# One fp32 product instead of three split products in the RG-LRU block of a two-network kernel

## The chip, the cores and the metric

The kernel runs on one core of one Trainium2 chip, as one program. The metric is the time of one execution in device microseconds (us). Five engines of the core matter here: PE (TensorE, the matrix engine; PEld is its weight load), DVE (VectorE), ACT (ScalarE), POOL (GpSimd), and SP (SyncE), whose queue issues most DMA transfers. Each engine takes its instructions strictly in program order, and semaphores hold one engine until another has done something.

## The reference, cut to what matters

The whole computes two networks one after the other, with 512 rows of 1024 numbers between them: a first block (a state-space mixer and an MLP), then two layers, each a mixer and a mixture of experts (MoE). The change touches the mixer of the very last layer, `mixer_rglru`:

```python
def mixer_rglru(h, w_in, conv_w, conv_b, w_a, b_a, w_x, b_x, lam, w_out):
    gate, xr = jnp.split(h @ w_in, [D_RNN], axis=-1)          # 512x1024 @ 1024x2048
    gate = jax.nn.gelu(gate)
    xr = causal_conv(xr, conv_w) + conv_b                      # 4 taps
    xh = xr.reshape(bsz, t_len, LRU_HEADS, LRU_HEAD_DIM)       # 8 heads of 128
    r = sigmoid(einsum('bthi,hij->bthj', xh, w_a) + b_a)
    i = sigmoid(einsum('bthi,hij->bthj', xh, w_x) + b_x)
    log_a = (LRU_C * r) * log_sigmoid(lam)
    a = exp(log_a)
    b = sqrt(-expm1(2.0 * log_a)) * (i * xr)
    hseq = scan of  h_t = a_t * h_(t-1) + b_t
    return (gate * hseq) @ w_out
```

All inputs and the output are fp32.

## The kernel before

PE takes its operands in two forms here. With plain fp32 operands a product is one instruction in the program. With operands of type fp32r the program first splits each operand into a high part (a rounded copy) and a low part (what is left), and makes three products of the parts, high x high, high x low and low x high (`mm3`, lines 265 to 267; the split of weights is `split`, L293 on ACT for the high part, L297 on DVE or L295 on POOL for the low part). The RG-LRU block works with the split form throughout.

The block lies between the MoE of the layer before it and its own output projection. At the end of that MoE, `over` transposes the first half of the 512 rows (`gT`, PE L400, ACT L402 for the high part `nh`, DVE L404 for the low part `nl`). Then 16 views follow. A view is one column block of 128 outputs by 512 rows: eight products of 128x128 by 128x512 summed in one PSUM bank, over the eight chunks of 1024. The first two views are one item, done in halves, with the other four transposes between the halves (`hook`). Eight views make the recurrent input x (m = 0 to 7) and eight make the gate (m = 8 to 15), in the order that a list sets:

```python
order = [0, 1, 2, 3, 8, 4, 9, 5, 10, 6, 11, 7, 12, 13, 14, 15]
```

After each view its callback `cb(i)` writes instructions for the other engines. For an x view (`cb_x`): a multiply out of PSUM by the row norm `rb`, and the four-tap convolution on DVE (L1746, L1749, three times L1751). `rb` is made once, at the end of the first two views, by `bcast_r` (PE L1669, ACT L1670). Later steps of a view are entered in the list `steps` at its own index plus an offset: `gates(m)`, which makes the two gate products of head m on PE and their Tanh and Exp on ACT; `middle(m)` (three DVE and two POOL operations, L1721 to L1725); `coef` (L1730 to L1736), `scan` (L1741) and `out`, which writes the block's result, split into `mh` and `ml`, for the output projection. `gates(m)` is not run at once but put into `k.fills`: five products steps into the next view its matmuls are written between those of that view, so they stand in PE's queue there. Before `gates` the kernel splits x (`copy_x` on ACT L1758, `sub_x` on DVE L1763).

Weights come by DMA through two buffers of 2 MB (pool `raw`): four chunks of four views each (`cols4`), the gate weights (`loadg`, split in `prepg`, POOL L1700), then two chunks of the output projection. The next chunk is issued when a buffer has been read for the last time; in the kernel before that reader is the split of its last view. Up to three splits are written ahead of their use. The output projection (`out_proj`, `tm_items`) keeps the three-product form, with splits L293 and L297. Behind it come routing and the MoE of the last layer.

Of the kernel before, what the change touches and what calls it, by code (L numbers as in the profile page):

```python
# [21 lines left out]
F32 = mybir.dt.float32  # L22
F32R = mybir.dt.float32r
# [8 lines left out]
P = 128  # L32
D = 1024
SEQ = 512
# [4 lines left out]
KD = D // P  # L39
# [12 lines left out]
GE = 7  # L52
# [9 lines left out]
def dram(ap, offset, dims):  # L62
    return bass.AP(tensor=ap.tensor, offset=ap.offset + offset, ap=dims)
# [54 lines left out]
class Kern:  # L118
# [35 lines left out]
    def pair(self, name, n):  # L154

        x = [self.slot(name, i, (4, n), F32R) for i in range(4)]
        return Rows(x[:2]), Rows(x[2:])
# [1321 lines left out]
class Second:  # L1479
# [175 lines left out]
    def rglru_open(self):  # L1655
        k = self.k
        p = self.np_ = k.open("abn")
        self.nh = p.tile([P, KD, SEQ], F32R, name="nh")
        self.nl = p.tile([P, KD, SEQ], F32R, name="nl")
        self.rb = p.tile([P, SEQ], F32, name="rb")  # L1660
        self.rr = p.tile([P, NB], F32, name="rr")
        self.g1 = k.g_mix2[:, 8:16]
# [9 lines left out]
    def rglru(self):  # L1672


        k = self.k
        v, s, t, g, A = k.v, k.s, k.t, k.g, k.A
        name = "c_w_in_2"
# [14 lines left out]
                k.nc.sync.dma_start(w[:, i], A[n].rearrange("o h i j -> i (o h) j"))  # L1692
            return w
        def prepg():
            w = k.piece(self.wg)
            self.wgh = self.np_.tile([P, 2, 8, P], F32R, name="wgh")
            self.wgl = self.np_.tile([P, 2, 8, P], F32R, name="wgl")
            for i in range(2):
                s.copy(self.wgh[:, i], w[:, i])
                g.tensor_sub(self.wgl[:, i], w[:, i], self.wgh[:, i].bitcast(F32))  # L1700
        W = lambda n, bufs, shape=(SEQ,), dt=F32: self.w.tile([P, *shape], dt, name=n, bufs=bufs)
        st, wait, held = {}, [], []

        def gates(m):
            x, xs = st[m]
            r = []
            for i in range(2):
                p = k.acc()
                k.mm3(p, self.wgh[:, i, m], self.wgl[:, i, m], xs[:, 0], xs[:, 1], True, True)
                o = W(f"r{i}", 2 + 2 * i)  # L1710
                s.activation(o, p, AF.Tanh, scale=0.5, bias=self.hb[:, i, m:m + 1])
                r.append(o)
            t1, t2 = r
            q = self.qs[:, m]
            s.activation(q, t1, AF.Exp, scale=self.cl[:, 2, m:m + 1], bias=self.cl[:, 2, m:m + 1])
            s.activation(self.hs[:, m], t1, AF.Tanh, scale=self.cl[:, 0, m:m + 1], bias=self.cl[:, 0, m:m + 1])
            st[m] = (x, t1, t2, q)

        def middle(m):
            x, t1, t2, q = st[m]  # L1720
            v.tensor_scalar(q, q, 1.0, None, op0=OP.add)  # L1721
            v.scalar_tensor_tensor(t1, self.hs[:, m], 1.0, q, op0=OP.add, op1=OP.mult)
            v.scalar_tensor_tensor(q, t1, 4.0, q, op0=OP.subtract, op1=OP.mult)
            g.tensor_mul(t2, t2, x)
            g.tensor_add(t2, t2, x)  # L1725
            st[m] = (q, t2)

        def coef(ms):
            for m in ms:
                s.activation(self.hs[:, m], self.hs[:, m], AF.Sqrt)  # L1730
            for m in ms:
                rec, i2 = st[m]
                h = self.hs[:, m]
                v.scalar_tensor_tensor(h, h, -0.25, rec, op0=OP.mult, op1=OP.mult)
                g.tensor_mul(i2, i2, h)
                v.tensor_scalar(rec, rec, -0.5, 1.0, op0=OP.mult, op1=OP.subtract)  # L1736

        def scan(ms):
            for m in ms:
                rec, i2 = st.pop(m)  # L1740
                v.tensor_tensor_scan(self.hs[:, m], rec, i2, 0.0, op0=OP.mult, op1=OP.add)  # L1741

        def cb_x(m, p):
            xr = W("xr", 2, (SEQ + 3,))
            v.memset(xr[:, 0:3], 0.0)
            v.tensor_mul(xr[:, 3:], p, self.rb)  # L1746
            x = W("xc", 4)
            c = k.c_conv
            v.tensor_scalar(x, xr[:, 0:SEQ], c[:, 0, m:m + 1], k.c_conv_b[:, m:m + 1], op0=OP.mult, op1=OP.add)  # L1749
            for i in (1, 2, 3):  # L1750
                v.scalar_tensor_tensor(x, xr[:, i:i + SEQ], c[:, i, m:m + 1], x, op0=OP.mult, op1=OP.add)  # L1751
            st[m] = (x,)
            wait.append(m)

        def copy_x(m):
            x, = st[m]
            xs = W("xs", 2, (2, SEQ), F32R)
            s.copy(xs[:, 0], x)  # L1758
            st[m] = (x, xs)

        def sub_x(m):
            x, xs = st[m]
            v.tensor_sub(xs[:, 1], x, xs[:, 0].bitcast(F32))  # L1763

        def cb_g(m, p):
            y = st["g", m] = W("y", 4)
            v.tensor_mul(y, p, self.rb)
            held.append(y)
            if m not in GP:
                for y in held:  # L1770
                    s.activation(y, y, AF.Gelu_apprx_tanh)
                held.clear()
# [7 lines left out]
        def beside(f, m):  # L1780
            for _ in range(FK):
                yield 1
            f(m)

        order = [0, 1, 2, 3, 8, 4, 9, 5, 10, 6, 11, 7, 12, 13, 14, 15]
        steps = [[] for _ in range(21)]
        at = {}
        for i, m in enumerate(order):
            if m < 8:
                o = 1 if i >= GE else 2  # L1790
                steps[i + o].append(lambda m=m, j=i + o: k.fills.append(beside(gates, m)) if j < FL else gates(m))
                steps[i + o + 1].append(lambda m=m: middle(m))
                if m % 2:
                    steps[i + o + 2].append(lambda m=m: coef((m - 1, m)))
                    steps[i + o + 3].append(lambda m=m: scan((m - 1, m)))
                    at[m - 1] = at[m] = i + o + 3
        for i, m in enumerate(order):
            if m >= 8:
                if m - 8 in GP:
                    i = order.index(m + 1)  # L1800
                steps[max(i + 1 if m - 8 in GP else i + 2, at[m - 8])].append(lambda m=m: out(m - 8))

        def cb(i, outs):
            p = outs[0][0]
            m = order[i]
            if i == 0:
                st["first"] = outs
                return
            ready = wait[:]
            wait.clear()  # L1810
            for x in ready:
                copy_x(x)
            if i == 1:
                self.bcast_r(self.rr, self.rb)
                cb_x(order[0], st.pop("first")[0][0])
                prepg()
            if i == 4:
                pass
            if m < 8:
                cb_x(m, p)  # L1820
            for x in ready:
                sub_x(x)
            for f in steps[i]:
                f()
            if m >= 8:
                cb_g(m - 8, p)
        tail = []

        def hook(j):
            if j == 0:  # L1830
                tail.append(k.gT(k.X, self.g1, self.nh, self.nl, range(4, KD)))
            next(tail[0]), next(tail[0])
            if j == 0:
                self.squares(k.sst[:, 0, 3], W("xs", 2, (2, SEQ)).rearrange("p i t -> p (i t)"))
            else:
                k.rstd(self.rr, k.sst[:, 0, 3], D, 1e-6, self.np_)

        def cols4(ms):
            src = A[name]
            return lambda: k.wload([(lambda w, i=i: w[:, :, i * P:(i + 1) * P],  # L1840
                                     dram(src, (D + P * m) % (2 * D), [[2 * D, P], [2 * D * P, KD], [1, P]]))
                                    for i, m in enumerate(ms)], (KD, 512))
        for i in range(4):
            k.fm_items(cols4(order[4 * i:4 * i + 4]), self.views(4 * i), self.acts, SEQ, cb, hook=None if i else hook,
                       pooled=range(4) if i else (2, 3))
            if i == 0:
                wg = self.wg = k.load(loadg, 1)
                wg.hold = True

        def late(k0):  # L1850
            for f in steps[16 + k0 // 2]:
                f()
# [391 lines left out]
    def moe(self, layer):  # L2244


        k = self.k
        v, s, t, g, A = k.v, k.s, k.t, k.g, k.A
# [184 lines left out]
        def over():  # L2433
            k.close("moew")
            k.close("rawx")
            k.close("rawn")
            k.close("xgp")
            k.close("tabl")
            k.close("rawm")
            k.close("tabs")  # L2440
            k.room.update(rawm=0, rawn=0, rawx=0)
            if not layer:
                self.wg.hold = False
                self.rglru_open()
                for _ in k.gT(k.X, self.g1, self.nh, self.nl, range(4)):
                    pass
                k.pump()
            k.dump(f"x{layer + 1}", k.X)
# [185 lines left out]
```

## Time and profile before

| | |
|---|---|
| median of 3 runs | 2319.97 us (2318.93 to 2323.73) |
| the profiled execution's own time | 2319.77 us |
| its span (first to last instruction) | 2318.0 us |
| PE busy | 2146.8 us, 11750 matmul records |
| DVE busy | 1120.5 us |
| ACT busy | 624.2 us |
| POOL busy | 305.7 us |
| mean granted TensorE clock | 0.968 |
| the stretch of the 16 views | from 1593.93 to 1744.96 us of the span |

Busy time of PE counts overlapping matmuls once, and matmul ends are modelled, so the distance from start to start of two matmuls in a stream says what one costs. One product with fp32 operands shows as two records of PE (and two weight loads); a product with fp32r operands as one. A row with a bracket names the idle time of the engine ahead of it and the instruction that ended it. The clock is given as a share of 2.4 GHz; the chip grants either that or 1.2 GHz.

### The profile page before, as it was taken

What the parts mean: (1) busy time and instruction counts of PE and PEld (TensorE: products, weight loads), DVE (VectorE), ACT (ScalarE), POOL (GpSimd) and SP (SyncE); (2) the same over time, 40 slices, a digit from 0 to 9 for tenths busy, and PEclk for the clock granted to TensorE, in tenths of its full rate; (3) what the DMA queues carried; (4) which work ended last, traced back from release to release, by engine and by line L of the source; (5) the groups of instructions that cost most, each with busy time, mean ns of one, the idle gap of its engine ahead of it and who ended that gap; (6) DMA issues with size and microseconds to landing.
All of it is one profiled execution on the core that took longest, in us unless ns stands there. A gap on an engine that the chain in (4) does not pass through costs nothing. (4 is left out here: it accounts for less than half of the span.)

```text
span 2318.0 us, 29809 instructions
## 1 busy us (share of the span) xinstructions
PE 2146.8 (93%) x11750; PEld 1368.8 (59%) x11750; DVE 1120.5 (48%) x2021; ACT 624.2 (27%) x961; POOL 305.7 (13%) x313
## 2 busy tenths in 40 slices
PE   6979999899999999998899999998769699999996
PEld 6868977778888888887333333345657333333332
DVE  6899556764443444555333322226975533222223
ACT  4333453333332333423111111112453211111111
POOL 2580003200000000011100000002550200000000
PEclk9988999999999999999899999998979799999998
DMA  8513343232332232326899999994315699999995
GB/s 204 126 44 101 100 128 101 63 118 82 109 109 87 95 109 73 109 73 247 350 425 425 426 426 426 426 409 125 83 55 225 263 425 425 425 426 426 426 418 208
DMA packets 152985, 540.25 MB, mean 233 GB/s; under 512 B 40421, under 2 KB 76505, under 8 KB 129161
## 3 DMA queue, kind: packets, MB, share of 16 engines
q1 hardware_dynamic: 135400, 516.19, 57.2%
q10 hardware_dynamic: 11680, 10.59, 1.5%
q0 software_dynamic: 5760, 11.52, 1.4%
q8 instruction: 94, 1.54, 0.3%
q14 instruction: 51, 0.41, 0.1%
HBM read 535.08 MB, written 11.57 MB: 236 GB/s over the span
## 5 line engine op out<-in xcount | busy, mean ns | idle before, releaser
L2324 PE MATMUL acc<-raw,wh 128*32 128x512 f32 (+1 forms) x2944 | 504.8, 598 | 13.8 <-DMA raw<-in_moe_w_up_dram 11.4
L2324 PEld LDWEIGHTS acc<-raw,wh 128*32 128x32 f32 (+1 forms) x2944 | 153.3, 120 | 302.7 <-issue 238.8
L2411 DVE TENSOR_TENSOR X<-X,sacc 128x512 f32<-128x512 f32 x245 | 156.8, 681 | 328.2 <-PE sacc L2409 328.2
L297 DVE TENSOR_TENSOR wl<-raw,wh 128x1024 fp32r<-128x1024 f32 x163 | 205.0, 1261 | 173.7 <-ACT wh L293 170.7
L293 ACT CAST wh<-raw 128x1024 fp32r<-128x1024 f32 x177 | 183.4, 1040 | 224.2 <-PE acc L266 127.9
L2324 PE MATMUL acc<-raw,hT 128*32 128x512 f32 (+1 forms) x1472 | 226.6, 594 | 1.4 <-ACT hT L2241 1.4
L265 PE MATMUL acc<-N,wh 128*128 128x264 f32 (+2 forms) x584 | 202.3, 346 | 0.0
L267 PE MATMUL acc<-N,wh 128*128 128x264 f32 (+2 forms) x584 | 193.6, 331 | 0.0
L266 PE MATMUL acc<-N,wl 128*128 128x264 f32 (+2 forms) x584 | 193.5, 331 | 0.0
L2324 PEld LDWEIGHTS acc<-raw,hT 128*32 128x32 f32 (+1 forms) x1472 | 67.4, 120 | 143.3 <-issue 132.1
L2399 DVE SCALAR_TENSOR_TENSOR wl<-acc,gs,wl 128x512 fp32r<-128x512 f32 x64 | 47.9, 751 | 183.1 <-ACT wl L2398 179.2
L2218 POOL DMA_INDIRECT xg<-hn_d,idx x32 | 31.9, 996 | 722.6 <-PE trp L2240 665.4
L265 PE MATMUL acc<-wh,N 128*128 128x512 f32 x288 | 123.6, 429 | 1.9 <-ACT N L1226 1.4
L265 PEld LDWEIGHTS acc<-N,wh 128*128 128x128 f32 (+1 forms) x584 | 110.4, 189 | 14.0 <-issue 0.7
L266 PEld LDWEIGHTS acc<-N,wl 128*128 128x128 f32 (+1 forms) x584 | 110.1, 189 | 10.6 <-issue 0.7
L267 PEld LDWEIGHTS acc<-N,wh 128*128 128x128 f32 (+1 forms) x584 | 109.9, 188 | 10.2
L266 PE MATMUL acc<-wh,N 128*128 128x512 f32 x288 | 115.0, 399 | 0.6 <-DVE N L1227 0.6
L267 PE MATMUL acc<-wl,N 128*128 128x512 f32 x288 | 115.1, 400 | 0.0
L2408 PE MATMUL sacc<-wl,oT 128*128 128x512 f32 x245 | 112.5, 459 | 1.1 <-DVE X L2411 1.1
L265 PE MATMUL acc<-wh,B 128*128 128x512 f32 x272 | 108.4, 399 | 0.0
L267 PE MATMUL acc<-wl,B 128*128 128x512 f32 x272 | 107.6, 395 | 0.0
L266 PE MATMUL acc<-wh,B 128*128 128x512 f32 x272 | 107.5, 395 | 0.0
(610 smaller groups left out, 3346.3 us busy)
## 6 DMA issues: line engine op xcount, KB each, us to landing
raw<-in_moe_w_gate_dram SPq DMA_DIRECT2D x64, 2048.0 KB, 25.0
raw<-in_moe_w_up_dram SPq DMA_DIRECT2D x60, 2048.0 KB, 28.2
raw<-in_moe_w_down_dram SPq DMA_DIRECT2D x60, 2048.0 KB, 25.5
raw<-in_w_up_dram SPq DMA_DIRECT2D x8, 2048.0 KB
raw<-in_w_down_dram SPq DMA_DIRECT2D x8, 2048.0 KB, 7.7
raw<-in_w_in_dram SPq DMA_DIRECT2D x7, 2048.0 KB, 11.5
raw<-in_ab_w_in_dram SPq DMA_DIRECT2D x5, 2048.0 KB
raw<-in_w_glu_dram SPq DMA_DIRECT2D x4, 2048.0 KB
```

What stands on the lines that cost most here:

```text
L265: t.matmul(out, ah, bh, start=start, stop=False)
L266: t.matmul(out, al, bh, start=False, stop=False)
L267: t.matmul(out, ah, bl, start=False, stop=stop)
L293: self.s.copy(wh, src)
L297: self.v.tensor_sub(wl, src, wh.bitcast(F32))
L2218: k.g.indirect_dma_start(out=xg, out_offset=None, in_=self.hn_d, in_offset=bass.IndirectOffsetOnAxis(ap=col, axis=0), bounds_check=SEQ - 1 ...
L2324: t.matmul(out[a:a + n], lhs[:, c, a:a + n], w[:, c, cols], start=start, stop=stop)
L2399: v.scalar_tensor_tensor(yl[:, sl], p[j], gs, yh[:, sl].bitcast(F32), op0=OP.mult, op1=OP.subtract)
L2408: t.matmul(p, oT[:, n * P:(n + 1) * P], yh[:, sl], start=True, stop=False)
L2411: v.tensor_add(x, x, p)
```

## The change

In the RG-LRU block nothing is split any more. The rows are one fp32 tile `nf` (no `nl`, so no DVE L404), the weights are used from the DMA buffer as they came, the gate weights are copied to `wgf` by two ACT copies (the POOL subtractions go), x goes into the gate products as it is (no `copy_x` or `sub_x`), and each `mm3` becomes one fp32 product. The items `pair` and `view` replace `fm_items`; a view holds its weight chunk until its products are done (`k.free(w)` after the fourth). `gates(m)` is entered one step earlier for m = 0 to 4. The output projection is as before; its splits may be written ahead only after item 12 (`fence`).

```diff
-        self.nh = p.tile([P, KD, SEQ], F32R, name="nh")
-        self.nl = p.tile([P, KD, SEQ], F32R, name="nl")
+        self.nf = p.tile([P, KD, SEQ], F32, name="nf")
...
         def prepg():
-            w = k.piece(self.wg)
-            self.wgh = self.np_.tile([P, 2, 8, P], F32R, name="wgh")
-            self.wgl = self.np_.tile([P, 2, 8, P], F32R, name="wgl")
+            w = k.whole(self.wg)
+            self.wgf = self.np_.tile([P, 2, 8, P], F32, name="wgf")
             for i in range(2):
-                s.copy(self.wgh[:, i], w[:, i])
-                g.tensor_sub(self.wgl[:, i], w[:, i], self.wgh[:, i].bitcast(F32))
+                s.copy(self.wgf[:, i], w[:, i])
+            k.free(self.wg)
...
-                k.mm3(p, self.wgh[:, i, m], self.wgl[:, i, m], xs[:, 0], xs[:, 1], True, True)
+                t.matmul(p, self.wgf[:, i, m], x, start=True, stop=True)
...
-        def copy_x(m):
-            x, = st[m]
-            xs = W("xs", 2, (2, SEQ), F32R)
-            s.copy(xs[:, 0], x)
-            st[m] = (x, xs)
-
-        def sub_x(m):
-            x, xs = st[m]
-            v.tensor_sub(xs[:, 1], x, xs[:, 0].bitcast(F32))
...
-                o = 1 if i >= GE else 2
+                o = 1
                 steps[i + o].append(lambda m=m, j=i + o: k.fills.append(beside(gates, m)) if j < FL else gates(m))
...
-            ready = wait[:]
-            wait.clear()
-            for x in ready:
-                copy_x(x)
...
-            for x in ready:
-                sub_x(x)
...
-                tail.append(k.gT(k.X, self.g1, self.nh, self.nl, range(4, KD)))
+                tail.append(k.gT(k.X, self.g1, self.nf, None, range(4, KD)))
...
+        def part(p, w, j, ks):
+            w = k.whole(w)
+            for c in ks:
+                t.matmul(p, w[:, c, j * P:(j + 1) * P], self.nf[:, c], start=c == 0, stop=c == KD - 1)
+                k.fill()
+
+        def pair(w):
+            ps = [k.acc(), k.acc()]
+            for j in range(2):
+                part(ps[j], w, j, range(KD // 2))
+                hook(j)
+            for j in range(2):
+                part(ps[j], w, j, range(KD // 2, KD))
+                cb(j, [(ps[j], 0, SEQ)])
+
+        def view(w, i):
+            p = k.acc()
+            part(p, w, i % 4, range(KD))
+            k.fill_end()
+            if i % 4 == 3:
+                k.free(w)
+            cb(i, [(p, 0, SEQ)])
         for i in range(4):
-            k.fm_items(cols4(order[4 * i:4 * i + 4]), self.views(4 * i), self.acts, SEQ, cb, hook=None if i else hook,
-                       pooled=range(4) if i else (2, 3))
+            w = k.load(cols4(order[4 * i:4 * i + 4]), 1)
             if i == 0:
                 wg = self.wg = k.load(loadg, 1)
                 wg.hold = True
+                k.add(lambda w=w: pair(w))
+            for j in range(4 * i + 2 * (i == 0), 4 * i + 4):
+                k.add(lambda w=w, j=j: view(w, j), fence=j == 12)
...
-                for _ in k.gT(k.X, self.g1, self.nh, self.nl, range(4)):
+                for _ in k.gT(k.X, self.g1, self.nf, None, range(4)):
```

The first place is PE around the first gate products, those of head 0. In the kernel before they stand five steps of three products into the fourth view, and the rows show the fifth step, the gates, and the sixth step (`xs` is the split x, `wgh` and `wgl` the split gate weights; a word in brackets ending in `_49` is a semaphore that the row waits on).

```order
L265 MATMUL acc<-nh,wh 128x512
L266 MATMUL acc<-nh,wl 128x512
L267 MATMUL acc<-nl,wh 128x512
L265 MATMUL sacc<-xs,wgh 128x512 [waits Activation_49]
L266 MATMUL sacc<-xs,wgl 128x512
L267 MATMUL sacc<-xs,wgh 128x512 [waits DVE_49]
L265 MATMUL sacc<-xs,wgh 128x512
L266 MATMUL sacc<-xs,wgl 128x512
L267 MATMUL sacc<-xs,wgh 128x512
L265 MATMUL acc<-nh,wh 128x512
```

In the changed kernel they stand one view earlier, in the third view, right behind the broadcast of the row norm (L1668), and read the convolved x itself (`xc`).

```order
L1668 MATMUL trp<-ident,rr 128x128 [waits DVE_49,PE_49]
L1668 MATMUL trp<-ident,rr 128x128 x3
L1825 MATMUL acc<-nf,raw 128x512 x5
L1707 MATMUL acc<-xc,wgf 128x512 [waits DVE_49,Activation_49]
L1707 MATMUL sacc<-xc,wgf 128x512 [waits Activation_49]
L1825 MATMUL acc<-nf,raw 128x512 x3
L1825 MATMUL sacc<-nf,raw 128x512 x5
L1707 MATMUL acc<-xc,wgf 128x512 [waits DVE_49]
L1707 MATMUL acc<-xc,wgf 128x512
L1825 MATMUL sacc<-nf,raw 128x512 x3
```

So six split products became two, the gates wait for DVE's convolution where they waited for ACT's copy and DVE's subtraction, and only five fp32 products lie between the broadcast and the first gate.

The second place is SP's queue from the gate weights to the output projection (`in_c_w_in` are the chunks of the views, four transfers each; `in_c_w_out` those of the output projection). Before:

```order
L1692 DMA raw<-in_c_w_x_dram 128x8x128
L311 DMA raw<-in_c_w_in_dram 128x8x128 [waits DMAHW5_49,DMAHW4_49,Pool_49]
L311 DMA raw<-in_c_w_in_dram 128x8x128 x3
L311 DMA raw<-in_c_w_in_dram 128x8x128 [waits DVE_49,Pool_49]
L311 DMA raw<-in_c_w_in_dram 128x8x128 x3
L311 DMA raw<-in_c_w_in_dram 128x8x128 [waits DMAHW6_49,DMAHW1_49,DMAHW7_49,DMAHW0_49,Pool_49]
L311 DMA raw<-in_c_w_in_dram 128x8x128 x3
L311 DMA raw<-in_c_w_out_dram 128x8x512 [waits DMAHW4_49,DMAHW3_49,DMAHW5_49,DMAHW2_49,Pool_49]
L311 DMA raw<-in_c_w_out_dram 128x8x512 [waits DMAHW6_49,DMAHW1_49,DMAHW7_49,DMAHW0_49,Pool_49]
```

Now:

```order
L1691 DMA raw<-in_c_w_x_dram 128x8x128
L311 DMA raw<-in_c_w_in_dram 128x8x128 [waits DMAHW5_49,DMAHW4_49,Activation_49]
L311 DMA raw<-in_c_w_in_dram 128x8x128 x3
L311 DMA raw<-in_c_w_in_dram 128x8x128 [waits PE_49]
L311 DMA raw<-in_c_w_in_dram 128x8x128 x3
L311 DMA raw<-in_c_w_in_dram 128x8x128 [waits DMAHW6_49,DMAHW1_49,DMAHW7_49,DMAHW0_49,PE_49]
L311 DMA raw<-in_c_w_in_dram 128x8x128 x3
L311 DMA raw<-in_c_w_out_dram 128x8x512 [waits DMAHW4_49,DMAHW3_49,DMAHW5_49,DMAHW2_49,PE_49]
L311 DMA raw<-in_c_w_out_dram 128x8x512 [waits DMAHW6_49,DMAHW1_49,DMAHW7_49,DMAHW0_49,PE_49]
```

The order of the transfers is the same; the second chunk now waits for ACT's copies of the gate weights, and all later ones for PE's own last read of the buffer in place of POOL's last split.

## Rows read from the trace of the kernel before

**Rows 1.** Page, part 1: busy time of each engine, share, instructions.

```profile
PE 2146.8 (93%) x11750; PEld 1368.8 (59%) x11750; DVE 1120.5 (48%) x2021; ACT 624.2 (27%) x961; POOL 305.7 (13%) x313
```

**Rows 2.** Stretches: busy us and count of each engine, granted clock, DMA share, GB/s.

```profile
1440.00:1460.00 20.00, 19.18 (x82) 7.46 (x80) 6.83 (x13) 2.26 (x4) 0.99 (x1) 1.00 1.01 425
...
1593.93:1744.96 151.03, 116.95 (x458) 91.79 (x457) 123.50 (x138) 72.28 (x96) 73.62 (x39) 0.86 0.25 70
...
1607.88:1744.96 137.08, 103.00 (x393) 80.20 (x392) 115.17 (x116) 66.64 (x86) 73.62 (x39) 0.85 0.27 77
```

**Rows 3.** Timeline of PE, an fp32 product (L1616) in a split stream.

```profile
970.30 1.02 PE L1616 MATMUL acc<-vv,ws 128*128 128x512 f32 x2
970.76 0.80 PE L265 MATMUL acc<-N,wh 128*128 128x512 f32 x1
971.39 0.39 PE L266 MATMUL acc<-N,wl 128*128 128x512 f32 x1
...
976.40 0.40 PE L267 MATMUL acc<-N,wh 128*128 128x512 f32 x1
```

**Rows 4.** Timeline of PE in the MoE, fp32 products of 64 columns.

```profile
1573.48 7.09 PE L2324 MATMUL acc<-raw,hT 128*64 128x512 f32 x32
```

**Rows 5.** Waits from 1586 to 1830 us: total, times, longest.

```profile
PE acc L265 <- ACT xs L1758: 11.6, 2, 8.8
...
PE sacc L267 <- DVE xs L1763: 7.2, 2, 6.0
...
PE acc L266 <- POOL wl L295: 6.2, 2, 4.1
...
PE sacc L265 <- ACT xs L1758: 5.0, 1, 5.0
```

**Rows 6.** Timeline of PE after a wait, the first gate of m = 6.

```profile
1705.68 0.80 PE L265 MATMUL acc<-xs,wgh 128*128 128x512 f32 x1 [2.77 <-ACT xs L1758]
...
1710.22 0.63 PE L267 MATMUL sacc<-nl,wh 128*128 128x512 f32 x1
1710.65 0.63 PE L265 MATMUL sacc<-nh,wh 128*128 128x512 f32 x1
```

**Rows 7.** Timeline of DVE, two x views.

```profile
1609.59 0.69 DVE L1746 TENSOR_TENSOR xr<-acc,rb 128x512 f32<-128x512 f32 x1 [3.14 <-ACT rb L1670]
...
1610.90 8.30 DVE L1751 SCALAR_TENSOR_TENSOR xc<-xr,va,xc 128x512 f32<-128x512 f32 x3
...
1650.71 0.68 DVE L1746 TENSOR_TENSOR xr<-acc,rb 128x512 f32<-128x512 f32 x1
...
1652.08 2.33 DVE L1751 SCALAR_TENSOR_TENSOR xc<-xr,va,xc 128x512 f32<-128x512 f32 x3
```

**Rows 8.** Timeline of POOL.

```profile
1610.58 5.32 POOL L1700 TENSOR_TENSOR wgl<-raw,wgh 128x1024 fp32r<-128x1024 f32 x2 [16.77 <-ACT wgh L1699]
```

**Rows 9.** Groups of instructions from 1586 to 1770 us, POOL's weight subtractions.

```profile
L295 POOL TENSOR_TENSOR wl<-raw,wh 128x1024 fp32r<-128x1024 f32 x14 | 36.8, 2628 | 139.3 <-ACT wh L293 139.3
```

**Rows 10.** Timeline of PE at the start of the block.

```profile
1587.80 1.09 PE L400 MATMUL trp<-ident,X 128*128 128x128 f32 x8 [2.35 <-DVEq L2507]
1592.31 1.97 PE L400 MATMUL trp<-ident,X 128*128 128x128 f32 x8 [3.42 <-DVE nl L404]
...
1607.88 1.05 PE L1669 MATMUL trp<-ident,rr 128*128 128x128 f32 x8
```

**Rows 11.** Timeline of SP's queue, the chunks behind the gate weights.

```profile
1615.93 35.43 SPq L311 DMA_DIRECT2D raw<-in_c_w_in_dram  x12
```

**Rows 12.** Timeline of ACT, splits of weights.

```profile
1587.55 2.94 ACT L293 CAST wh<-raw 128x1024 fp32r<-128x1024 f32 x3 [6.25 <-DVEq L2507]
...
1620.25 1.04 ACT L293 CAST wh<-raw 128x1024 fp32r<-128x1024 f32 x1 [7.86 <-DMA raw<-in_c_w_in_dram]
```

**Rows 13.** Timeline of PE in the output projection.

```profile
1756.93 0.50 PE L265 MATMUL acc<-wh,mh 128*128 128x512 f32 x1 [0.61 <-ACT wh L293]
...
1758.20 0.50 PE L267 MATMUL acc<-wl,mh 128*128 128x512 f32 x1 [0.53 <-DVE wl L297]
```

More of the change, by code (lines that the diff above doesn't have):

```diff
@@ L1694, in prepg @@
         def prepg():
-            w = k.piece(self.wg)
-            self.wgh = self.np_.tile([P, 2, 8, P], F32R, name="wgh")
-            self.wgl = self.np_.tile([P, 2, 8, P], F32R, name="wgl")
+            w = k.whole(self.wg)
+            self.wgf = self.np_.tile([P, 2, 8, P], F32, name="wgf")
             for i in range(2):
-                s.copy(self.wgh[:, i], w[:, i])
-                g.tensor_sub(self.wgl[:, i], w[:, i], self.wgh[:, i].bitcast(F32))
+                s.copy(self.wgf[:, i], w[:, i])
+            k.free(self.wg)
         W = lambda n, bufs, shape=(SEQ,), dt=F32: self.w.tile([P, *shape], dt, name=n, bufs=bufs)
-        st, wait, held = {}, [], []
+        st, held = {}, []
         def gates(m):
-            x, xs = st[m]
+            x, = st[m]
             r = []
@@ L1752, in cb_x @@
             st[m] = (x,)
-            wait.append(m)
-        def copy_x(m):
-            x, = st[m]
-            xs = W("xs", 2, (2, SEQ), F32R)
-            s.copy(xs[:, 0], x)
-            st[m] = (x, xs)
-        def sub_x(m):
-            x, xs = st[m]
-            v.tensor_sub(xs[:, 1], x, xs[:, 0].bitcast(F32))
         def cb_g(m, p):
@@ L1816, in cb @@
                 prepg()
-            if i == 4:
-                pass
             if m < 8:
                 cb_x(m, p)
-            for x in ready:
-                sub_x(x)
             for f in steps[i]:
```

## The prediction

> **What bounds the kernel now.** I read the page first. PE is busy 93% of the span and DVE only 48% [rows 1], but these are means over stages with different limits, so the question is what ends last in the stage that the change touches. The view by stretches answers that. In the MoE, DMA runs at a share of 1.01 and 425 GB/s, with PE nearly always busy and the clock granted at 1.00; the 16 views of the RG-LRU block, 151.03 us long, have DMA at 0.25, PE busy 116.95 and a clock of 0.86 [rows 2]. So the block is neither full of transfers nor full of matmuls.
>
> What would it take if PE never waited? In a split stream the 22 steps from 971.39 to 976.40 give 0.2277 us a product [rows 3]. The block has 144 products to make (16 views of eight, and 16 gate products), three split ones each: 432 x 0.2277 = 98.4 us. Some 53 us of the 151 are something else. The view of waits names the largest: PE waited 11.6, 7.2 and 5.0 us for the split x of a gate product (`xs`, from ACT and DVE), and 6.2 for POOL's low part of a weight chunk [rows 5]. Behind such a wait the matmuls come slower for a while: after the wait that ends at 1705.68, two neighbours at 1710.22 and 1710.65 are still 0.43 apart in place of 0.23 [rows 6], which is the lower of the two clock levels (1.2 in place of 2.4 GHz).
>
> Why is x late? DVE was busy 115.17 of the 137.08 us behind the first two views [rows 2], and its operations stretch when POOL works. The three convolution steps of an x took 8.30 us beside POOL's 5.32 us subtraction of gate weights and what followed, and 2.33 us undisturbed [rows 7, 8]. POOL spent 36.8 us on weight subtractions [rows 9].
>
> **What is removed.** All splits go: POOL's 14 weight subtractions in this block and the two of gate weights, DVE's low parts of rows, weights and x, ACT's casts of them. None is worth its own duration; what they are worth is the PE waits above, which end.
>
> **What is added: the price of an fp32 product.** The nearest row has the same shape, 128x128 by 128x512. L1616 starts at 970.30, its two records are listed together, and the L266 two products later starts at 971.39. One split step before that is 971.16: 0.862 us for one fp32 product. (L265 is listed from 970.76, but lasts 0.80 where others last 0.39: it stood behind the fp32 records.) [rows 3] The other bound is the MoE, where 32 records, two side by side and so eight steps, took 7.09 us with the tail of the last: 0.886 [rows 4]. I take 0.862, the same shape. Against 3 x 0.2277 = 0.683 each product costs 0.179 more, 144 of them 25.8 us.
>
> The Trainium skill, page "FP8 and Floating Point Precision", section "TensorE Precision Notes", says that a true fp32 product goes through the array in four passes, which speaks against replacing three products by one. Its four passes, each priced as a split product, would be 4 x 0.2277 = 0.911, 7 us more over the block than the row's 0.862; the row decides.
>
> **The new path, step by step.** Times are those of the old trace, as if nothing ahead had changed.
>
> Start. PE made the first eight transposes at 1587.80 and waited 3.42 us for DVE's `nl` before the next eight at 1592.31 [rows 10]; ACT, meanwhile, did 2.94 us of weight casts before it evicted [rows 12]. Neither is left, so the first product moves from 1593.93 [rows 2] to about 1590.5; if ACT's evictions hold it, at most back to 1591.5.
>
> First two views: 16 x 0.862 = 13.8, two lots of eight transposes at up to 1.09 [rows 10], and 0.7 for a short stretch at the lower level (bounds 0 and 1.3; PE waits less than before, so I take the middle). They end at 1590.5 + 13.8 + 2.2 + 0.7 = 1607.2; before, the broadcast behind them started at 1607.88 [rows 10]. The earlier start has paid for the dearer products.
>
> First gate. It now stands five products behind the broadcast: 1.05 + 5 x 0.862 = 5.4 us after the broadcast starts. Its x: DVE began 1609.59 - 1607.88 = 1.7 us after the broadcast [rows 7, 10], and one x undisturbed takes from 1650.71 to 1652.08 + 2.33, 3.7 us [rows 7], and POOL has nothing to do then. That is 5.4 too: no wait that matters. ACT's two copies of gate weights (about 1 us each by the casts [rows 12]) run beside the convolution.
>
> Later gates. A head's gates come 11 us or more behind the end of its x view (a rest of 4.3 in their own view, and a whole view of 6.9 between, where gates of another head add 1.7). The x takes 3.7 to 9.6 us (the longer one from 1609.59 to the end of 8.30 [rows 7]), behind what DVE's queue holds. I allow 1 us in all.
>
> Weights. The second chunk waits for ACT's copies, not POOL's subtraction: about 4.3 us after the broadcast. Issued at 1615.93, it let ACT go on at 1620.25 [rows 11, 12], 4.3 us, so it is there 9 us behind the broadcast and is wanted at 18. SP has nothing between it and the gate weights. Later chunks wait for PE's last read of a buffer and are wanted four views, 27 us, later. The cover is those views; without it each chunk would cost its 4.3 us. The first splits of the output projection come with view 13, three at once, under some 20 us of products.
>
> Sum. 1607.2 + 1.05 for the broadcast + 128 products (14 views, 16 gates) x 0.862 = 110.3 + 1 of allowance = 1719.6, against 1744.96 before [rows 2]: 25.4 us. In the output projection PE waited 0.61 and 0.53 us for splits of weights that ACT and DVE got to late [rows 13]; now they are early: 1.1. Together 26.5. The rest (projection, routing, MoE) starts that much earlier and keeps its length: its transfers can start only when pools close late in the projection, so they move along. The profiled execution took 2319.77 us, its span 2318.0 and 1.8 around it, 0.2 under the median; 2319.8 - 26.5 = **2293.3 us**.
>
> **The rivals.**
>
> *Four passes at the price of split products.* A product then costs 0.911: 144 x 0.049 = 7.1 more, 2300.4. Against it stand both rows of fp32 streams.
>
> *x still late.* If DVE keeps the pace of before, its 115 us are as much as PE's 111 behind the first two views, and x of heads 5 to 7, behind a scan and an output in DVE's queue, misses its gates. A wait as in [rows 6] is 2.77 us, and 5 us at double spacing lose another 2.3. Two or three of them are 10 to 15, less the 1 allowed: 2302 to 2307. POOL's remaining work speaks for it (73.62 less 36.8 and 5.32, so 31 us [rows 2, 8, 9]); that the greater part of what stretches DVE is gone speaks against.
>
> *Slower: PE at the lower level.* A product there costs twice 0.862. The gain is gone when 26.5 / 0.862 = 31 of the 144, 21%, run there. Before, a clock of 0.86 [rows 2] means 28% of the stretch at that level, so this isn't far off; half of the products there would give 2293.3 + 62 = 2355. Against it: the lower level follows waits here, these go, and the MoE's fp32 stream had 1.00 [rows 2].
>
> *Nothing arrives.* If the last MoE's transfers were tied to something that doesn't move, the time stays 2320. DMA at 0.25 in the block [rows 2] shows no such stream running ahead.
>
> **How the numbers follow.** The forecast, with its bounds, gets 0.62: 2290.3 at the bottom (start 0.3 earlier, neither 0.7 nor 1), 2297 at the top (0.886 for a product). Four passes 0.08, late x 0.17, lower clock 0.05, nothing arrives 0.03; 0.05 is for less than 2290. The shown runs reach from 1 under their median to 4 over it. The range 2288.5 to 2306 takes in forecast, four passes and most of late x, about 8 in 10. A measurement of this kernel can tell some 0.2% from no change, here 4.6 us; all cases but the last two of the rivals lie beyond that on the faster side: faster 0.92, same 0.03, slower 0.05.
>
> **What would show it right or wrong.** Right: the view products two records each, some 0.43 apart; from first product to the output projection some 129 us, PE busy nearly all of it, clock 0.95 or more; the first product some 3 us behind the start of the first transposes; no wait of PE on ACT's or POOL's splits; convolution steps mostly near 2.3 us for three. Wrong, and how: waits of PE for `xc` above 2 us, with lower clock behind them (late x); gaps at the first view of a chunk (the buffers held too long); product spacing of 0.9 or more at full clock; or the block shorter and the gap behind it longer.

## The result, and the profile after

The changed kernel took 2292.55 us (median of 4 runs, 2287.90 to 2295.60), the kernel before beside it 2320.64: 0.9876 of its time, 95% interval 0.9856 to 0.9896. Measured again later on another occasion it took 2290.76 (2288.70 to 2292.45) against 2321.52, 0.9874 (0.9855 to 0.9894). So it is 28 to 31 us faster, and 2293.3 had been predicted. The profiled execution took 2287.9 us and was the fastest of its four, so its trace shows a somewhat larger gain than the median.

First the view by stretches of the changed kernel, as in [rows 2]: from the first product to the output projection, and from the broadcast on.

```profile
1588.85:1715.08 126.23, 126.08 (x314) 57.03 (x313) 86.03 (x128) 58.69 (x78) 34.17 (x24) 1.00 0.27 73
1604.34:1715.08 110.74, 110.59 (x265) 49.28 (x264) 82.80 (x112) 53.08 (x68) 34.17 (x24) 1.00 0.28 76
```

PE is busy in all but 0.15 us of the stretch and its granted clock is 1.00 where it was 0.86. Behind the broadcast POOL is down from 73.62 to 34.17 us and DVE from 115.17 to 82.80. PE alone sets the length of the block now. Then PE's timeline there, which answers to [rows 3, 10, 13].

```profile
1586.35 1.09 PE L400 MATMUL trp<-ident,X 128*128 128x128 f32 x8 [2.35 <-DVEq L2510]
1587.78 1.24 PE L400 MATMUL trp<-ident,X 128*128 128x128 f32 x8 [0.34 <-ACT nf L402]
1588.85 3.60 PE L1825 MATMUL acc<-nf,raw 128*128 128x512 f32 x8
...
1604.34 1.05 PE L1668 MATMUL trp<-ident,rr 128*128 128x128 f32 x8
1605.23 4.46 PE L1825 MATMUL acc<-nf,raw 128*128 128x512 f32 x10
1609.84 1.10 PE L1707 MATMUL acc<-xc,wgf 128*128 128x512 f32 x2
...
1639.95 11.32 PE L1825 MATMUL acc<-nf,raw 128*128 128x512 f32 x26
1651.11 1.88 PE L1707 MATMUL sacc<-xc,wgf 128*128 128x512 f32 x4
...
1715.08 0.79 PE L265 MATMUL acc<-wh,mh 128*128 128x512 f32 x1
```

The wait for `nl` (3.42) has become one of 0.34. The 26 records from 1639.95 end where the gate starts, 11.16 us later: 13 products of 0.858 us, two records each. The first gate product (1609.84) has no bracket, but the ten records ahead of it, 0.429 us each from 1605.23, end at 1609.52: PE lost 0.32 us there. DVE's row of the three convolution steps shows that x was ready at 1609.69, and that the steps take 2.33 us where they took 8.30 [rows 7]:

```profile
1607.36 2.33 DVE L1749 SCALAR_TENSOR_TENSOR xc<-xr,va,xc 128x512 f32<-128x512 f32 x3
```

The waits of PE that are listed from 1580 to 1760 us, the whole answer:

```profile
PE trp L400 <- DVEq L2510: 2.3, 1, 2.3
PE trp L400 <- ACT nf L402: 0.3, 1, 0.3
PE acc L2412 <- DVE wl L2402: 0.3, 1, 0.3
PE acc L265 <- DVE X L1888: 0.2, 1, 0.2
```

Against [rows 5], all waits for `xs` and for POOL's `wl` are gone. From the first transposes to the output projection there are 128.73 us in place of 157.16, 28.43 less; from there to the first product of the MoE 79.04 in place of 80.77; 1.45 had come ahead of the block and 0.29 came behind the first product of the MoE. These sum to the 31.9 us between the two spans.

### The profile page after: what moved, and what is told of

Read it like the earlier page. It is cut to its first block, busy times and chain, and to the rows that moved or that the text cites. A ratio compares the mean times of both kernels' runs of the same rounds, so it can differ in the third digit from the quotient of the medians.

```text
span 2286.1 us, 29447 instructions
## 1 busy us (share of the span) xinstructions
PE 2155.5 (94%) x11606; PEld 1328.8 (58%) x11606; DVE 1075.7 (47%) x2003; ACT 605.3 (26%) x937; POOL 261.6 (11%) x297
## 5 line engine op out<-in xcount | busy, mean ns | idle before, releaser
L2327 PEld LDWEIGHTS acc<-raw,wh 128*32 128x32 f32 (+1 forms) x2944 | 148.4, 120 | 305.9 <-issue 243.8
L293 ACT CAST wh<-raw 128x1024 fp32r<-128x1024 f32 x161 | 166.8, 1040 | 214.6 <-PE acc L266 127.9
L2221 POOL DMA_INDIRECT xg<-hn_d,idx x32 | 31.9, 997 | 722.4 <-PE trp L2243 693.7
```

Source lines behind the costliest of these rows:

```text
L293: self.s.copy(wh, src)
L2221: k.g.indirect_dma_start(out=xg, out_offset=None, in_=self.hn_d, in_offset=bass.IndirectOffsetOnAxis(ap=col, axis=0), bounds_check=SEQ - 1 ...
L2327: t.matmul(out[a:a + n], lhs[:, c, a:a + n], w[:, c, cols], start=start, stop=stop)
```

## The experiments

Distances below run from the start of the first transposes to the first product of the output projection ("the block"), and from there to the first MoE product ("behind it"). They are free of shifts ahead of the block, which vary between executions: in the profiles here the first transposes start anywhere from 1581.43 to 1590.04. The changed kernel has 128.73 and 79.04. A `...` in a cut of code stands for lines left out.

**The changed kernel again.**

> The changed kernel itself once more, on the chip of the two kernels below, for a comparison with them. 2288 to 2296 us, ratio to the kernel before 0.985 to 0.990. Its profile also tells whether PE's clock stays at 1.00 from the second lot of transposes on, as in the first profile of it, or whether the second lot takes 1.7 to 1.95 us and the first eight records 4.5 to 4.8, as in e1, e2 and e4.

2290.76 us, as expected; the block 130.34, behind it 78.95. The 1.6 us more in the block are the lower clock level at its start:

```profile
1588.92 1.69 PE L400 MATMUL trp<-ident,X 128*128 128x128 f32 x8 [0.34 <-ACT nf L402]
1590.40 4.79 PE L1825 MATMUL acc<-nf,raw 128*128 128x512 f32 x8
```

These rows are 0.45 and 1.19 us longer than the same ones above, behind the same waits; the granted clock in them is 0.66 and 0.74, and 1.00 in the first profile. The term of 0.7 us in the prediction for this is 0 in one execution and 1.6 in another.

**Gates one step later.**

```diff
-                o = 1
+                o = 1 if i >= GE else 2
```

> The changed kernel, with the early heads' gates entered one step later again, as in the kernel before. Theory (the gain came from the splits that are gone, and PE has no wait for x in either order): same time as the changed kernel, 2290 to 2296 us, PE without a wait for x in the block, block some 126 us from first product to output projection. Rival (the earlier gates brought part of the gain, through the scans and outputs that follow them): 2297 us or more, with the output projection waiting for the last heads' outputs.

2288.82 us (2286.46 to 2292.76), ratio 0.9864 (0.9849 to 0.9879); block 129.88, behind it 78.74, no wait for x. The rival falls: entering the gates earlier brought nothing that can be seen, and the two kernels can't be told apart.

**Only the gates in fp32.** The kernel before, with this edit, without `copy_x` and `sub_x`, and with the gate weights copied as in the change, so that POOL's two subtractions of them go too:

```diff
-                k.mm3(p, self.wgh[:, i, m], self.wgl[:, i, m], xs[:, 0], xs[:, 1], True, True)
+                t.matmul(p, self.wgf[:, i, m], x, start=True, stop=True)
...
-                o = 1 if i >= GE else 2
+                o = 1
```

> The kernel before, with only the gate products in fp32: x and the gate weights are no longer split, gates are entered one step after their view; rows and view weights are still split, POOL's 14 subtractions included. Theory (the waits for split x, 23.8 us of the three largest, were the main loss; the views' splits cost one wait of 6.2): PE's products sum to 128 x 0.683 + 16 x 0.858 = 101 us against 123.6 in the changed kernel, PE's waits for xs are gone, the one for POOL's low part stays, block 120 to 133 us from first product to output projection, 2288 to 2302 us. Rival (the stretched DVE is the loss, and it stays since POOL's work stays): PE waits for xc where it waited for xs, 2303 to 2315 us. Rival (the views' splits are the loss): 2312 us or more.

2301.24 us (2299.67 to 2302.40), ratio 0.9919 (0.9906 to 0.9933). Block 136.83. The waits for `xs` went; these are among the largest that were there instead, from 1580 to 1760 us:

```profile
PE acc L266 <- POOL wl L295: 3.9, 2, 2.1
PE trp L400 <- DVE nl L404: 3.4, 1, 3.4
PE acc L1707 <- DVE xr L1743: 3.1, 1, 3.1
PE sacc L1707 <- DVE xc L1749: 2.9, 1, 2.9
...
PE sacc L265 <- ACT wh L293: 2.3, 1, 2.3
```

Both the theory and its first rival have a part: the time lies in the theory's range, near its end, since 6.0 us of wait for x stayed, beside 6.0 for POOL's low parts and 5.2 for ACT's casts of weights.

**Only the views in fp32.** The changed kernel, with the gates' `mm3`, `copy_x`, `sub_x` and the later step put back.

> The changed kernel, with the gate products split again as in the kernel before: x and gate weights in high and low parts, gates two steps after their view; rows and view weights stay fp32. Theory (with POOL's weight subtractions gone and 6.9 us for a view, x and its parts are in time): PE's products sum to 128 x 0.858 + 16 x 0.683 = 121 us, at most a few us of PE waits for xs, 2290 to 2299 us. Rival (the split x is late whatever the views do, as long as gates are split): waits of 5 us or more for xs, 2303 us or more.

2302.87 us (2298.77 to 2303.03), ratio 0.9916 (0.9902 to 0.9929). Block 141.99. Here the theory failed: with POOL's 14 subtractions gone and 6.9 us for a view, the split x still came late, for the same two gates as the two longest waits of before.

```profile
PE acc L265 <- ACT xs L1758: 5.0, 1, 5.0
PE sacc L267 <- DVE xs L1763: 4.4, 1, 4.4
```

So the gates alone bring 19.8 us, the views alone 18.2, and both some 28 to 32: less than the sum of the two.

At the first gate of this run POOL's remaining 5.24 us with the gate weights still stretched the convolution, to 6.26 us, and x's low part stood in DVE's queue behind two more convolutions. Why is the split x late further on, where DVE has room? The answer stands in the kernel before, at its longest wait (head m = 5):

```profile
1688.53 0.80 PE L265 MATMUL acc<-xs,wgh 128*128 128x512 f32 x1 [8.84 <-ACT xs L1758]
```

First DVE's timeline, then ACT's:

```profile
1673.20 4.30 DVE L1751 SCALAR_TENSOR_TENSOR xc<-xr,va,xc 128x512 f32<-128x512 f32 x3
...
1680.64 1.75 DVE L1776 TENSOR_TENSOR y<-y,mh 128x512 f32<-128x512 f32 x1
```

```profile
1682.42 0.62 ACT L1496 CAST mh<-y 128x512 fp32r<-128x512 f32 x1 [6.39 <-DVE y L1776]
1682.95 1.04 ACT L293 CAST wh<-raw 128x1024 fp32r<-128x1024 f32 x1
1684.01 1.28 ACT L1711 ACT_TABLE_LOAD   x1
1685.30 0.69 ACT L1711 ACTIVATE r<-sacc,hb 128x512 f32<-128x512 f32 x1
...
1687.87 0.61 ACT L1758 CAST xs<-xc 128x512 fp32r<-128x512 f32 x1
```

x was ready at 1677.5, 2.2 us before PE began to wait. Its cast started 10.4 us later, because ACT's queue held, ahead of it, the cast of an earlier head's output that waited 6.39 us for DVE, then a weight cast, a table load and four activations of another head. The Trainium skill, page "Perfetto Trace Analysis", section "Tensor Engine Instruction (MATMUL, LD_WEIGHTS)", says that ACT and DVE work strictly first in, first out; these rows agree. A gate in fp32 reads `xc` itself and has no ACT instruction ahead of it.

The same wait in the run with only the views in fp32 is clearer still. The convolution is undisturbed there (first row, DVE) and x is ready at 1669.95, 5.0 us before PE begins to wait. Its cast starts 9.4 us later, again behind one that waits for DVE (the other rows):

```profile
1667.62 2.33 DVE L1751 SCALAR_TENSOR_TENSOR xc<-xr,va,xc 128x512 f32<-128x512 f32 x3
```

```profile
1674.85 0.62 ACT L1496 CAST mh<-y 128x512 fp32r<-128x512 f32 x1 [5.35 <-DVE y L1776]
...
1679.34 0.61 ACT L1758 CAST xs<-xc 128x512 fp32r<-128x512 f32 x1
```

No run moved the cast of x alone within ACT's queue.

**POOL's subtractions put back.** If the gain is that POOL no longer stretches DVE, it must go again when only POOL's work returns, to no purpose:

```diff
+        def low(src):
+            wl = k.whl.tile([P, 1024], F32R, name="wl", bufs=k.nwh)
+            g.tensor_sub(wl.rearrange("p (k n) -> p k n", k=8), src, src)
...
+                low(w[:, i])
...
+            low(k.whole(w)[:, :, i % 4 * P:(i % 4 + 1) * P])
```

> The changed kernel, with POOL's 14 weight subtractions and its two of gate weights put back as idle work into a scratch tile that nothing reads; PE's and ACT's work stays that of the changed kernel. Theory (POOL's splits stretched DVE, but DVE with no low parts of its own has room under PE's fp32 products): DVE's busy time in the block rises from 83 to 95 or 105 us, POOL's from 34 to some 70, three convolution steps that meet POOL take 4 to 8 us again, yet the time rises only 0 to 5 us (2291 to 2298). Rival (the whole gain is that DVE is no longer stretched): x is late again, PE waits 3 us or more for an xc several times, and the time is 2303 us or more.

2301.05 us (2298.33 to 2301.59), more than the theory's number, but not as the rival has it: block 130.33 without a wait for x; behind it 89.80 in place of 79.04. PE waited there for a late output, and POOL's timeline says why:

```profile
1738.21 0.80 PE L265 MATMUL acc<-wh,mh 128*128 128x512 f32 x1 [5.67 <-ACT mh L1496]
```

```profile
1724.23 1.89 POOL L1695 TENSOR_TENSOR wl<-raw 128x1024 fp32r<-128x1024 f32 x1 [26.30 <-PE sacc L267]
```

The scratch tile came from the ring that the output projection's splits use; POOL stood 26.30 us until PE had read one, with the last heads' work queued behind. This is a flaw of the experiment, so it was made again with a tile of its own:

```diff
-            wl = k.whl.tile([P, 1024], F32R, name="wl", bufs=k.nwh)
-            g.tensor_sub(wl.rearrange("p (k n) -> p k n", k=8), src, src)
+            g.tensor_sub(self.scr.rearrange("p (k n) -> p k n", k=8), src, src)
...
+            self.scr = self.np_.tile([P, 1024], F32R, name="scr")
```

> As e2_pool_subs_back (POOL's weight subtractions of 14 views and of the gate weights put back as idle work into a tile that nothing reads), but with a scratch tile of their own. In e2 they wrote into tiles that the output projection's splits share, and one of them waited 26.30 us for a matmul of that projection, with POOL's work for the last head behind it. Theory 1 (that shared tile made e2's 8 us): no such wait, no PE wait for mh, time within 3 us of the changed kernel, 2289 to 2296 us, though DVE's busy time stays near that of e2. Theory 2 (the stretched DVE itself makes the last heads' outputs late): PE waits for mh again, 2298 us or more.

2294.39 us (2292.64 to 2295.79), 1.8 and 3.6 us above the two measurements of the changed kernel. The stretch behind the broadcast:

```profile
1606.15:1716.89 110.74, 110.60 (x266) 49.28 (x264) 98.60 (x106) 49.18 (x63) 58.65 (x34) 1.00 0.28 76
```

DVE is 16 us busier than in the changed kernel, and the stretch has the same 110.74 us: PE covers all of it. Only behind the block, 83.73 in place of 79.04, small waits of 0.2 to 1.4 us for splits and outputs show that DVE ended later; one of 0.75 is for `mh`, where theory 1 had none. By the time theory 1 holds, with two limits. Nothing here waits for ACT's casts, so POOL did the gate weights' two from 1592 to 1598, ahead of the first convolution, and their collision with it [rows 7, 8] isn't in this run. And the run tells what POOL's work costs beside fp32 products, not what it cost in the kernel before, where PE's products were shorter.

**A kernel that beats both?** An fp32 product costs 0.175 us more than three split ones, so views would rather be split, as far as ACT, DVE and POOL can feed them. Six kernels tried it.

> As e3_only_gates_fp32 (views still split, gates fp32), but the low parts of the view weights are made by DVE, none by POOL. Theory (in e3 what is left above the changed kernel is POOL: its low parts come late, and they stretch the convolution): PE has 101 us of products in place of 123.5; DVE's convolution falls from 41.5 us to 19 to 25 and gains 14 subtractions of 1.22 us, so DVE has 83 + 17 + 6 = 106 us and is the bound; waits of PE for wl from POOL are gone; time 2284 to 2296 us. Rival (DVE has no room for 17 us more): waits for wl from DVE and for xc grow, 2299 us or more.

(`pooled`, the list of views whose low parts POOL makes, is empty here, in the kernel with only the gates in fp32.) 2295.63 us (2289.57 to 2296.90), at the upper end of the theory's range. Block 129.55, behind it 84.25. The products are 22 us shorter than in the changed kernel and the block is not: the waits for `nl` (4.6), for ACT's weight casts (6.1 in all, 1.7 of it behind the block) and for DVE's low parts ate it. No engine was full: of 108.74 us behind the broadcast PE was busy 97.78 and DVE 95.22, so DVE was not the bound that the theory made it.

The others keep the rows in fp32 and split them as well, and split only some views:

```diff
+                for c in range(KD):
+                    s.copy(self.nh[:, c], self.nf[:, c])
+                    g.tensor_sub(self.nl[:, c], self.nf[:, c], self.nh[:, c].bitcast(F32))
...
-                k.add(lambda w=w, j=j: view(w, j), fence=j == 12)
+                if i in (1, 2):
+                    k.add(lambda ws, j=j: sview(ws, j),
+                          lambda w=w, j=j: k.split(k.piece(w)[:, :, j % 4 * P:j % 4 * P + P], (KD, P), g if j in () else None))
+                else:
+                    k.add(lambda w=w, j=j: view(w, j), fence=j in (2, 12))
```

(`sview` makes eight `mm3` with these parts; `xs` has one buffer here, for room. In `if j in ()` stand the views whose low parts POOL makes: none.)

> The changed kernel, with views 4 to 11 in split products again: rows kept in fp32 and also split (high parts by ACT after the squares, low parts by POOL), low parts of these eight weights by DVE; views 0 to 3, 12 to 15 and all gates in fp32. Theory (an fp32 product costs 0.175 us more than a split one, and DVE, idle 28 of the 111 us behind the first two views, can take eight subtractions of 1.22 us): PE's products fall by 64 x 0.175 = 11.2 us, and if at most 4 us of new PE waits come, 2280 to 2287 us. Rival (the room of DVE isn't where it is needed): waits for wl or xc eat the gain, 2289 us or more.

2287.57 us (2285.84 to 2288.53), ratio 0.9852 (0.9835 to 0.9868): between theory and rival. Block 127.29. Of 11.2 us some 8 went into waits, among them

```profile
PE sacc L265 <- ACT wh L293: 2.2, 1, 2.2
PE acc L1709 <- DVE xr L1745: 1.7, 1, 1.7
PE acc L1709 <- DVE xc L1751: 1.4, 1, 1.4
```

> As h8_mixed_views, with views 4 to 15 split. Theory: 96 x 0.175 = 16.8 us less of products, 12 subtractions on DVE (14.7 us) bring it to 98 us of some 94 that PE needs: DVE becomes the bound at the end, where the last heads' outputs are due; 2277 to 2288 us. Rival (DVE's end sets the time): PE waits 5 us or more for mh or X at the end, and it is slower than h8.

With `(1, 2, 3)`: 2296.62 us (2292.24 to 2297.65). Block 130.23, behind it 83.29, where the output projection waited for its weights' casts (longest 1.48). Slower than h8, as the rival has it, though not by waits for `mh`.

> h8_mixed_views with the early heads' gates one step later again. In h8 PE waited 3.3 us for xc and xr at three gate products, and 4.7 for parts of weights, and the products behind a wait came at half pace for a while. Theory (with faster views the slack of x is what fp32 views gave; a step later gives it back): no wait at a gate product, 3 to 6 us less than h8, 2281 to 2286 us. Rival (DVE's queue is late as a whole, and the wait moves to the weights' low parts or to the end): same as h8, 2286 to 2290 us.

2290.54 us (2283.69 to 2294.43), past both ranges, and its runs are too far apart to place it above or below h8. Block 130.10. The gates' waits all but went (one of 1.24 is left), and one of 4.42 came at a view, for a PSUM tile that ACT had not yet read, behind the cast of an output that waited 7.28 us for DVE, as above. So the wait moved, though not to a place that the rival names:

```profile
1670.31 0.50 PE L265 MATMUL sacc<-nh,wh 128*128 128x512 f32 x1 [4.42 <-ACT r L1711]
```

> As h8_gates_later, with the low parts of the eight split views' weights by POOL in place of DVE. Theory (e6 showed that POOL's subtractions cost at most 2 us where PE has slack over DVE): DVE is relieved of 9.8 us, PE's waits for wl move to POOL or vanish; 2279 to 2286 us. Rival (with split products the slack is gone, as in e3, where PE waited 6 us for POOL's low parts and 6 for xr and xc): 2287 us or more.

2293.74 us (2286.56 to 2297.46), in the rival's range. Block 134.97. The wait for low parts moved from DVE to POOL (6.3 us in all) and grew.

Apart from 1.7 us at the first gate, which the later gates remove, PE's waits in these begin at 1647 to 1655 us, when the second split chunk comes up. So the last kernel splits the first of them only, views 4 to 7, with `i in (1,)` and the gates later:

> As h8_gates_later, but only views 4 to 7 are split. In h8_gates_later PE's first wait of the mixed stretch came at 1649.62, with views 8 and later; views 4 to 7 and their gates had none. Theory (mixing pays as long as no wait of PE comes with it): products fall by 32 x 0.175 = 5.6 us against the changed kernel and no wait is added; from the first transposes to the output projection 123 to 125 us against 128.7 and 130.3 in the two profiles of the changed kernel, time 2283 to 2287 us. Rival (DVE's and ACT's four splits push the later heads' work back, and the wait comes later): 127 us or more, 2288 us or more.

2285.74 us (2280.55 to 2287.16), ratio 0.9844 (0.9827 to 0.9861). Block 123.96, behind it 78.83, the listed waits in the block 0.3 us or less:

```profile
1589.16 1.09 PE L400 MATMUL trp<-ident,X 128*128 128x128 f32 x8 [2.34 <-DVEq L2528]
...
1679.97 1.96 PE L1709 MATMUL acc<-xc,wgf 128*128 128x512 f32 x4 [0.26 <-DVE xc L1751]
...
1713.12 0.79 PE L265 MATMUL acc<-wh,mh 128*128 128x512 f32 x1
```

The theory's numbers came out. All five runs lie below all eight of the changed kernel, and the block is 4.8 us shorter than in its first profile, which also has the full clock at the start. So the changed kernel is beaten by some 5 to 7 us between the medians. The two were not timed side by side, and their ratios to the kernel before (0.9827 to 0.9861, and 0.9856 to 0.9896 and 0.9855 to 0.9894) overlap by a little.

## Why the prediction was right, and where it was not

- **Price of an fp32 product.** 0.862 taken, 0.858 measured over whole views: 0.5 us over the block. The rival of four passes at the price of split products fell: 0.858 is 3.77 times the 0.2277 of a split product. How often the array is passed, no row here shows.
- **Start.** From the first transposes to the first product 2.70 us predicted; 2.50 and 2.92 in the two profiles.
- **First two views.** 16.7 predicted, 15.49 and 16.68 measured. The whole difference of the two is the clock, the term of 0.7, which differs from execution to execution. Beside it, a lot of eight transposes was put at 1.09, its duration; from start to start it takes 0.87, so the two lots are 0.4 too dear.
- **From the broadcast to the output projection.** 112.4 predicted, 110.74 in both profiles. Of the 1 us for late x 0.3 was needed, at the first gate; the broadcast was shorter by 0.2, the products by 0.5, and the projection's first row is listed some 0.4 us early (it is 0.79 long, as others are behind fp32 records).
- **Output projection.** 1.1 us predicted; the stretch behind the block is 1.7 and 1.8 shorter as listed, some 0.4 more by the remark above. The wait of 0.75 us for `X` there, which the sum did not hold, fell to 0.23.
- **Sum.** 26.5 predicted, 28.1 and 30.8 between the medians. But for the clock's, every mis-sized term erred toward less gain, by a few tenths to 0.7 us each. In the two profiles the block and the stretch behind it are together 30.2 and 28.6 us shorter than before. That the first median lies only 0.75 us from 2293.3 is thus in part luck.
- **Range of the forecast.** Its bottom, 2290.3, doesn't follow from the terms named for it: 2293.3 - 0.3 - 0.7 - 1 is 2291.3. One median lies above that and one below, so the gain was a little underrated.
- **The other rivals.** The lower clock level is gone behind the broadcast (1.00, from 0.85), no gate waits more than 0.32 us for x, and the time did move.
- **The step that is only half right** is the reason given for late x: "DVE was busy 115.17 of the 137.08 us behind the first two views [rows 2], and its operations stretch when POOL works." The sum didn't rest on it, but the rival "x still late" did. By the rows of before it holds at the first gate (5.98 us), where stretched convolutions stand ahead of x's low part, and at m = 6 (2.77), where three steps took 6.13 us and x was cast at once. At m = 5 (8.84) and m = 7 (5.03) x was ready 2.2 and 1.8 us before PE began to wait, and stood in ACT's queue behind a cast that waited for DVE. What that cast waited for had stretched operations ahead of it, too, so there the two causes don't come apart: with POOL's weight subtractions gone and views longer, 5.05 of the 8.84 us stayed, and how the other 3.8 and the wait at m = 7 divide was not tried.
- **What it missed** is that an fp32 gate drops the way through ACT's queue. In the changed kernel the runs give prices: POOL's subtractions put back cost 1.8 to 3.6 us; split gates put back, with the casts and low parts of x, POOL's two subtractions of gate weights and the later step, cost 10.3 to 12.1. The longer of the two waits for x that came back there, 5.05 us, followed an undisturbed convolution. So beside fp32 views the direct way is worth more than the stretch that POOL's subtractions cause. That it is so beside split views is not shown: with only the gates in fp32, 6 us of wait for x stayed.

## What to carry to other kernels

A split operand costs more than its casts: each of its parts joins an in-order queue and is as late as what stands there ahead of it; one dearer product that reads the value directly can be cheaper on an engine that was waiting. When an operand comes late, look at when its source was ready and at what its engine did until then, before blaming a busy or slowed engine. And after such a change PE is the bound, so the products' price counts again: put the cheaper form back where the feeding engines have room, chunk by chunk, and stop at the first wait.

## What was not expected of the hardware

- The same matmuls behind the same waits of 2.35 and 0.34 us ran at the full clock in one execution of the changed kernel (granted clock 1.00, 3.60 us for the first eight records) and partly at the lower level in the other (0.74, 4.79 us).
- Beside POOL, DVE's instructions lengthen by kind. DVE's timeline of the changed kernel, then POOL's:

```profile
1633.05 0.69 DVE L1732 SCALAR_TENSOR_TENSOR mh<-mh,ml 128x512 f32<-128x512 f32 x1 [4.56 <-ACT mh L1728]
...
1634.12 1.75 DVE L1732 SCALAR_TENSOR_TENSOR mh<-mh,ml 128x512 f32<-128x512 f32 x1
...
1636.25 1.50 DVE L1719 TENSOR_SCALAR ml<-ml 128x512 f32<-128x512 f32 x1
...
1641.03 0.68 DVE L1754 TENSOR_TENSOR y<-acc,rb 128x512 f32<-128x512 f32 x1
```

```profile
1633.82 1.51 POOL L1733 TENSOR_TENSOR r<-r,mh 128x512 f32<-128x512 f32 x1 [10.01 <-DVE mh L1732]
1636.02 1.45 POOL L1733 TENSOR_TENSOR r<-r,mh 128x512 f32<-128x512 f32 x1 [0.69 <-DVE mh L1732]
...
1640.52 1.72 POOL L1722 TENSOR_TENSOR r<-r,xc 128x512 f32<-128x512 f32 x1
```

An operation on two SBUF tiles takes 0.69 us alone and 1.75 beside POOL; one that reads an accumulator and one SBUF tile takes 0.68 beside POOL. The Trainium skill, page "SBUF — State Buffer", section "Who interferes with whom", has this rule: two SBUF inputs contend with POOL's reads; at most one doesn't, outside modes in which DVE uses both of its port pairs. These rows agree. The row of L1719 shows that one SBUF input isn't enough to be safe: it takes 0.42 us alone (at 1626.54) and 1.50 beside POOL. Whether it ran in such a mode no row shows.
